# Gate and up products of the narrow expert slots with channels striped over four partition blocks and transposed in 32x32 blocks on VectorE; another order of the expert slots

## The chip, the cores and the metric

The kernel runs on one core of a Trainium2 chip. The metric is the device time of one execution in microseconds (us), lower is better. All matrices are in float32. PE is TensorE, DVE is VectorE, ACT is ScalarE, POOL is GpSimd, and SP is SyncE, whose queue issues the weight transfers.

## The reference

Two layers of a streaming encoder for 256 tokens with 1024 channels. Each layer mixes tokens (convolution and attention, then an output projection), then applies a feed-forward part. In the first layer that is a dense SwiGLU, in the second a mixture of eight experts of which each token uses two. The part that matters here is the second layer's:

```python
def moe_swiglu(h, w_router, b_router, w_gate, w_up, w_down):
    t = h.reshape(B * S, D)                       # 256 x 1024
    logits = t @ w_router + b_router
    top_val, top_idx = lax.top_k(logits, TOP_K)   # 2 of 8
    top_w = jax.nn.softmax(top_val, axis=-1)
    combine = sum(one_hot(top_idx, 8) * top_w)    # 256 x 8
    for e in range(8):
        # w_gate[e], w_up[e]: 1024 x 3584, w_down[e]: 3584 x 1024
        out += combine[:, e] * ((silu(t @ w_gate[e]) * (t @ w_up[e])) @ w_down[e])
```

## The kernel before, in words

The weights of the eight experts are 352 MB and pass through the chip once; each token goes only through its own two experts. The stage after the router is a list of **units** that Python writes out, and the order of that list is the order on every engine (`manual_schedule`).

**Slots.** Experts are put into eight slots by their number of tokens, at run time. Slot `e` has room for `32 * CAPS[e]` tokens, with `CAPS = (3, 4, 3, 3, 3, 2, 2, 2)`, so a slot has 2, 3 or 4 **groups** of 32 tokens. Slot 1 has 128 tokens and is called **wide**; the other seven are narrow. Each slot has seven units (`N_DN`), one for every 512 of the 3584 expert channels.

**Lanes.** `LANES` names two sequences of slots. The first three units of the first lane's first slot stand alone (`STAGGER`), then units of the first and second lane alternate, and the last three units of the second lane stand alone at the end. So a unit of one slot has a unit of another as its neighbour, and I write 3+2 for a pair of a three-group and a two-group unit.

**One unit** (the loop at the end of `moe`): `gu_mm` multiplies the tokens by 512 gate and 512 up channels, takes silu on ACT and multiplies on DVE; `dn_mm` multiplies the unit before it by its 512 rows of the down matrix; `h_T` transposes the unit's product, so that the next round's `dn_mm` can use it as the stationary operand. PE therefore runs: gate and up of unit n, down of unit n-1, transposes of unit n, gate and up of unit n+1.

**Narrow units** use PE in four strips of 32 columns (`streams`, line 1089): the 32 tokens of a group are the stationary operand, the weights are the moving one, and strip j takes a fourth of the channels and writes partitions 32j to 32j+31 of a PSUM bank. Strips run at the same time. In `gu_mm` one matmul has 128 gate and 128 up channels, 256 columns. The trace shows two records for a float32 matmul. Since a strip holds 128 neighbouring channels, the product must be transposed as a whole 128x128 square for each group: one PE transpose a group (line 1130) into a PSUM bank, and one ACT copy to SBUF (line 1137).

**The wide unit** splits its weights into two parts of fewer bits (line 140 on ACT and line 148 on DVE) and uses full 128x128 matmuls in three terms (lines 254 to 256).

**The weight stream.** A unit brings six tiles of 1 MiB (128x2048 float32): four of gate and up, two of down. `plan` lists them, SP issues them in that order (line 131), and each waits for its buffer to be freed. Near the wide slot tiles lie in the nine buffers of the pool `raw`. Elsewhere they also use the three buffers each of `hi` and `lo`, 15 in all. A narrow unit's tile is freed by the matmuls that read it, a wide one's by DVE's pass at line 148.

**Around the units.** Before a slot's first unit its tokens are gathered by matmuls (`dispatch`, lines 1025 to 1078); after its last one `gated` and `combine` scale the result and scatter it back (lines 1164 to 1200).

Of the kernel before, what the change touches and what calls it, by code (L numbers as in the profile page):

```python
# [13 lines left out]
AF = mybir.ActivationFunctionType  # L14
ALU = mybir.AluOpType
AX = mybir.AxisListType

P = 128
# [3 lines left out]
KT = 8  # L22
# [12 lines left out]
SPARE4 = (1, 6, 8)  # L35
EARLY = 7
CAPS = (3, 4, 3, 3, 3, 2, 2, 2)
LANES = (0, 2, 1, 3), (5, 4, 6, 7)
STAGGER = 3
NR = NE - 1  # L40
EPS = 1e-6
# [12 lines left out]
def kernel(ctx, tc, x, cvec, wada, bada, wga, wqkv, wout, wfgu, wfd, wfd2,  # L54
                      wmgu, wmd, cols, bias, wrt, brt, out):
    nc = tc.nc
# [10 lines left out]
    def bank(name):  # L67
        return pb.tile([P, 512], F32, tag="b", name=name)
# [6 lines left out]
    def sized(tag):  # L75
        def f(name, shape, dt=F32):
            return pools["wk"].tile(shape, dt, tag=tag, name=name, bufs=bufs[tag])
        return f

    a8, a4, a2 = sized("a8"), sized("a4"), sized("a2")  # L80
# [70 lines left out]
    plan = []  # L151
# [11 lines left out]
    first_gu = len(plan)  # L163
    runs = [[(e, c) for e in lane for c in range(N_DN)] for lane in LANES]
    units = runs[0][:STAGGER]
    for u in zip(runs[0][STAGGER:], runs[1]):
        units += u
    units += runs[1][-STAGGER:]
    after = {e: n for lane in LANES for e, n in zip(lane, lane[1:])}
    order = {0: 0}  # L170

    def of_slot(w, e, *parts):

        def f(c, h):
            v = w[0, c] if e == 0 else w[bass.ds(order[e], 1), c].rearrange("o p n -> (o p) n")
            return v[:, h * G:h * G + G]
        return lambda: [f(*p) for p in parts]

    def wide(e):
        return CAPS[e] == 4  # L180

    def down_chunk(e, c):
        return of_slot(wmd, e, (c, 0), (c, 1)), 4096 if wide(e) else 0

    for i, (e, c) in enumerate(units):
        parts = [[(2 * c + a, h) for h in range(2)] for a in range(2)]
        plan += [(of_slot(wmgu, e, *p), 4096 if wide(e) else 0) for p in (parts if wide(e) else zip(*parts))]
        if i:
            plan.append(down_chunk(*units[i - 1]))
    plan.append(down_chunk(*units[-1]))  # L190
# [36 lines left out]
    def blk(la=2, pre=True):  # L227

        i = used[0]
        used[0] += 1  # L230
        ahead(max(0, i + 1 + la - len(his)), max(0, i + 1 + la - len(los)), pre)
        return his[i], los[i]
# [674 lines left out]
    def moe(acc, g_bc, mm, A, B, AW, bw):  # L907
# [105 lines left out]
        def slot_pick(e):  # L1013
            src = places if e else posm
            return pick(lambda t: src[:, t, e:e + 1], 32 * CAPS[e])
# [68 lines left out]
        def streams(ps, g, x, w, first, last):  # L1084


            for t in range(g):
                for j in range(4):
                    nc.tensor.matmul(ps[t // 2][32 * j:32 * j + 32, t % 2], x(t), w(j),  # L1089
                                     start=first and t % 2 == 0, stop=last, skip_group_check=True)  # L1090

        def gu_mm(e, between):


            g, xg = CAPS[e], disp[e][0]
            ps = [bank(f"ps_gu{b}") for b in range((g + 1) // 2)]
            if wide(e):
                for b in range(2):
                    for s in range(2):
                        w = blk(min(2, 3 - 2 * b - s))  # L1100
                        for i in range(4):
                            k = 4 * s + i
                            mm3(ps[b], (xg[:, 0, k, :], xg[:, 1, k, :]), [v[:, 512 * i:512 * i + 512] for v in w],
                                k == 0, k == KT - 1)
                pv = [p_.rearrange("p (u t s) -> p t u s", t=2, u=2) for p_ in ps]
            else:
                pv = [p_.rearrange("p (t u s) -> p t u s", t=2, u=2) for p_ in ps]
                for h in range(2):
                    w = whole(3)
                    for i in range(4):  # L1110
                        k = 4 * h + i
                        wk_ = [w(a, i).rearrange("p (u j s) -> p u j s", u=2, j=2) for a in range(2)]
                        streams(pv, g, lambda t: xg[:, k, 32 * t:32 * t + 32], lambda j: wk_[j // 2][:, :, j % 2],
                                k == 0, k == KT - 1)
            between()
            sg = a2("sg", [P, g, P])
            hm = a2("mh", [P, g, P])
            for b, v in enumerate(pv):
                m = min(2, g - 2 * b)
                nc.scalar.activation(sg[:, 2 * b:2 * b + m, :], v[:, 0:m, 0, :], AF.Silu)  # L1120
            for b, v in enumerate(pv):
                m = min(2, g - 2 * b)
                nc.vector.tensor_tensor(hm[:, 2 * b:2 * b + m, :], v[:, 0:m, 1, :], sg[:, 2 * b:2 * b + m, :],  # L1123
                                        op=ALU.mult)
            return hm

        def h_T(hm, g, split=False):
            ps = bank("ps_hT").rearrange("p (a s) -> p a s", a=4)
            for t in range(g):
                nc.tensor.transpose(ps[:, t, :], hm[:, t, :], ident)  # L1130
            if split:
                hT = [a2(n, [P, g, P], F32R) for n in ("hThi", "hTlo")]
                nc.scalar.activation(hT[0], ps, AF.Copy)
                nc.vector.tensor_tensor(hT[1], ps, hT[0].bitcast(F32), op=ALU.subtract)
            else:
                hT = a2("hT", [P, g, P])
                nc.scalar.activation(hT, ps[:, 0:g, :], AF.Copy)  # L1137
            return hT
# [154 lines left out]
        with tc.manual_schedule():  # L1293
            limit[0] = len(halves)
            for r in range(NR):
                order[r + 1] = nc.values_load(idx_i[0:1, r:r + 1], engines=[mybir.EngineType.SP], min_val=1, max_val=NR,
                                              skip_runtime_bounds_check_because="a rank's expert")
            g2r = const.tile([P, 256], F32, tag="crep", name="g2r")
            pend, done = None, []
            for n, (e, c) in enumerate(units):  # L1300
                early = [(pe, gated(pe)) for pe in done]
                done = []
                if c == N_DN - 2 and e in after:
                    nxt = after[e]
                elif n == STAGGER - 1:
                    nxt = LANES[1][0]
                else:
                    nxt = None
                if nxt is not None:
                    pm = slot_pick(nxt)  # L1310

                def between():
                    if pend and wide(pend[0]):
                        ahead(2)

                hm = gu_mm(e, between)
                if n == 1:
                    g2_bc = bcast(vec(1, 5), "g2bc")
                    dgs = [a2("dg", [P, 4, P]) for i in range(2)]
                    for i, dg in enumerate(dgs):  # L1320
                        nc.vector.tensor_tensor(dg, ident[:, None, :].to_broadcast([P, 4, P]),
                                                vec(1, 5)[:, 4 * i:4 * i + 4, None].to_broadcast([P, 4, P]), op=ALU.mult)
                    ps = bank("ps_g2")
                    for j in range(4):
                        nc.tensor.matmul(ps[32 * j:32 * j + 32, 0:256], ones_1[:, 0:32],
                                         dgs[j // 2][:, 2 * (j % 2):2 * (j % 2) + 2, :].rearrange("p a s -> p (a s)"),
                                         start=True, stop=True)
                    nc.scalar.activation(g2r, ps[:, 0:256], AF.Copy)
                for pe, ys in early:
                    if pe == 0:  # L1330
                        macc = a8("macc", [P, NT, D])
                    combine(pe, ys)
                if pend is not None:
                    if pend[1] == 0:
                        accs[pend[0]] = [accbank(f"ps_d{b}") for b in range((CAPS[pend[0]] + 1) // 2)]
                    dn_mm(*pend)
                    if pend[1] == N_DN - 1:
                        done.append(pend[0])
                if n + 1 < len(units) and wide(units[n + 1][0]):
                    ahead(2)  # L1340
                pend = e, c, h_T(hm, CAPS[e], wide(e))
                if nxt is not None:
                    disp[nxt] = dispatch(nxt, pm)
            for pe in done:
                combine(pe, gated(pe))
            dn_mm(*pend)
            combine(pend[0], gated(pend[0]), store)
# [164 lines left out]
```

## Time and profile before

| | |
|---|---|
| median of three runs | 1421.37 us (1417.27 to 1430.04) |
| the profiled execution | 1421.24 us, its span 1419.2 us |
| PE, PE weight loads | busy 1349.9 us (95%), 973.1 us (69%) |
| DVE, ACT | busy 565.3 us (40%), 398.4 us (28%) |
| DMA | 473.64 MB, mean 334 GB/s |
| expert stage | from 519.2 us to the end of the span |

The span is the time from the first to the last instruction on the core. An engine's busy time is the sum over the span, so it mixes stages with different limits. Matmuls overlap, and the end of each is modelled, so a busy PE need not be at its peak; the start of one stream of matmuls to the start of the next is the better measure of its pace. A stretch in which the DMA engines are busy all the time and one in which PE is can follow one another within a stage, and only a view by stretches tells them apart.

### The profile page before, as it was taken

How to read it: one execution, taken by the hardware profiler on the slowest of the kernel's cores; microseconds unless marked ns; L12 is line 12 of the kernel's file. 1: busy time of each engine (PE TensorE's matmuls, PEld its weight loads, DVE VectorE, ACT ScalarE, POOL GpSimd, SP SyncE). 2: the span in 40 equal slices, each digit the busy share in tenths (PEclk: the TensorE clock that was granted, in tenths of full speed). 3: DMA queues.
4: the chain of work that ended last, by engine and by line, in shares of the span. 5: the costliest groups of instructions: out<-in, count | busy, mean ns of one | idle time of the engine just before them, and what ended most of it. 6: DMA issues, size and time to landing. Idle time of an engine off the chain costs nothing.

```text
span 1419.2 us, 38942 instructions
## 1 busy us (share of the span) xinstructions
PE 1349.9 (95%) x17604; PEld 973.1 (69%) x17604; DVE 565.3 (40%) x1025; ACT 398.4 (28%) x635; POOL 3.0 (0%) x17
## 2 busy tenths in 40 slices
PE   4998899999899999999999999999999999999886
PEld 4877699999697686657666656677667766665453
DVE  3597677777689651000100100354455430010011
ACT  3335444433456330101001001334333420100000
POOL 0000000000000000000000000000000000000000
PEclk9999999999999999999999999999999999999998
DMA  9963787878551579899999995989898999999995
GB/s 383 418 243 123 263 308 273 305 272 307 172 205 45 206 292 369 342 417 417 417 417 417 417 417 223 396 350 362 327 379 346 397 417 417 417 417 417 417 418 202
DMA packets 66379, 473.64 MB, mean 334 GB/s; under 512 B 7840, under 2 KB 7968, under 8 KB 9248
## 3 DMA queue, kind: packets, MB, share of 16 engines
q1 hardware_dynamic: 66208, 471.09, 83.3%
q8 instruction: 140, 2.29, 0.6%
q14 instruction: 31, 0.25, 0.0%
HBM read 470.01 MB, written 1.05 MB: 332 GB/s over the span
## 4 chain that ended last, share of the span: by engine, by line
PE 77%; DMA 13%; DVE 5%; ACT 3%; issue 1%; SPq 0%; DVEq 0%; ACTq 0%
PE ps_gu L1089 23%; PE ps_d L1089 13%; DMA raw<-in_wmgu 6%; DMA raw<-in_wmd 6%; PE ps_ga L256 4%; PE ps_ga L254 4%; PE ps_ga L255 4%; PE ps_g L1025 2%; PE ps_y L708 2%; PE ps_gu L256 2%; PE ps_gu L254 2%; PE ps_gu L255 2%; DVE cv L544 2%; PE ps_ada L308 1%; DVE lo L148 1%; PE ps_hT L1130 1%
## 5 line engine op out<-in xcount | busy, mean ns | idle before, releaser
L1089 PE MATMUL ps_gu<-raw,xn 128*32 128x256 f32 x8064 | 450.2, 380 | 4.1 <-DMA raw<-in_wmgu 3.9
L1089 PEld LDWEIGHTS ps_gu<-raw,xn 128*32 128x32 f32 x8064 | 269.1, 110 | 169.2 <-DMA raw<-in_wmgu 7.8
L148 DVE TENSOR_TENSOR lo<-raw,hi 128x2048 fp32r<-128x2048 f32 x99 | 225.5, 2289 | 84.7 <-ACT hi L140 82.0
L1123 DVE TENSOR_TENSOR mh<-ps_gu,sg 128x256 f32<-128x256 f32 (+1 forms) x91 | 32.7, 382 | 547.2 <-ACT sg L1120 547.2
L1089 PE MATMUL ps_d<-raw,hT 128*32 128x256 f32 x4032 | 232.3, 381 | 8.0 <-DMA raw<-in_wmd 7.5
L140 ACT ACTIVATE hi<-raw 128x2048 fp32r<-128x2048 f32 x99 | 188.3, 1912 | 107.2 <-PE ps_ga L256 43.0
L1089 PEld LDWEIGHTS ps_d<-raw,hT 128*32 128x32 f32 x4032 | 133.7, 110 | 96.6 <-DMA raw<-in_wmd 9.9
L1120 ACT ACTIVATE sg<-ps_gu 128x256 f32<-128x256 f32 (+1 forms) x91 | 32.0, 352 | 426.3 <-PE ps_gu L1089 380.7
L254 PE MATMUL ps_ga<-hThi,lo 128*128 128x256 f32 x480 | 137.5, 287 | 7.6 <-ACT hThi L446 7.6
L256 PE MATMUL ps_ga<-hTlo,hi 128*128 128x256 f32 x480 | 136.9, 285 | 0.8 <-DVE hTlo L451 0.8
L255 PE MATMUL ps_ga<-hThi,hi 128*128 128x256 f32 x480 | 136.3, 284 | 0.0
L254 PEld LDWEIGHTS ps_ga<-hThi,lo 128*128 128x128 f32 x480 | 92.9, 194 | 8.7 <-ACT hThi L446 8.4
L256 PEld LDWEIGHTS ps_ga<-hTlo,hi 128*128 128x128 f32 x480 | 92.4, 192 | 1.4 <-DVE hTlo L451 1.4
L255 PEld LDWEIGHTS ps_ga<-hThi,hi 128*128 128x128 f32 x480 | 92.4, 193 | 0.2
L544 DVE SCALAR_TENSOR_TENSOR cv<-zp,cols_sb,cv 128x256 f32<-128x256 f32 x206 | 85.4, 477 | 0.0
L1137 ACT ACTIVATE hT<-ps_hT 128x384 f32<-128x384 f32 (+1 forms) x49 | 21.8, 445 | 221.4 <-PE ps_hT L1130 221.4
L347 DVE SCALAR_TENSOR_TENSOR ada_acc<-raw,cs,ada_acc 128x512 f32<-128x512 f32 x63 | 47.2, 749 | 1.2
L256 PE MATMUL ps_gu<-lo,xg 128*128 128x512 f32 x112 | 44.3, 396 | 1.3 <-DVE lo L148 1.3
L254 PE MATMUL ps_gu<-hi,xg 128*128 128x512 f32 x112 | 44.8, 400 | 0.0
L255 PE MATMUL ps_gu<-hi,xg 128*128 128x512 f32 x112 | 44.3, 396 | 0.0
L308 PE MATMUL ps_ada<-raw,crep 128*32 128x128 f32 x960 | 34.4, 302 | 7.4 <-DMA raw<-in_wada 7.1
L308 PEld LDWEIGHTS ps_ada<-raw,crep 128*32 128x32 f32 x960 | 29.2, 121 | 11.2 <-issue 8.3
(263 smaller groups left out, 1310.1 us busy)
## 6 DMA issues: line engine op xcount, KB each, us to landing
raw<-in_wmgu SPq DMA_DIRECT2D x222, 1024.0 KB, 13.9
raw<-in_wmd SPq DMA_DIRECT2D x111, 1024.0 KB, 14.3
raw<-in_wada SPq DMA_DIRECT2D x48, 1024.0 KB, 6.2
raw<-in_wfgu SPq DMA_DIRECT2D x22, 1024.0 KB, 6.0
raw<-in_wqkv SPq DMA_DIRECT2D x12, 1024.0 KB, 6.6
raw<-in_wfd SPq DMA_DIRECT2D x11, 1024.0 KB, 6.5
raw<-in_wga SPq DMA_DIRECT2D x8, 1024.0 KB, 10.6
raw<-in_wout SPq DMA_DIRECT2D x8, 1024.0 KB, 7.7
```

The source lines that it names most:

```text
L140: nc.scalar.activation(hi[:, i * w:(i + 1) * w], r, AF.Copy)
L148: nc.vector.tensor_tensor(lo[:, w], r, hi[:, w].bitcast(F32), op=ALU.subtract)
L254: nc.tensor.matmul(o_, a[1], b[0], start=first, stop=False)
L255: nc.tensor.matmul(o_, a[0], b[0], start=False, stop=False)
L256: nc.tensor.matmul(o_, a[0], b[1], start=False, stop=last)
L308: nc.tensor.matmul(ps[32 * g:32 * g + 32, 0:P], crep[:, j, :], w(j)[:, g * P:(g + 1) * P], start=j == 0, stop=j == KT - 1)
L347: nc.vector.scalar_tensor_tensor(accs[ch], ws[ch](j), cs[:, j:j + 1], accs[ch], op0=ALU.mult, op1=ALU.add)
L544: nc.vector.scalar_tensor_tensor(cv[:, a, :], zp[:, a, i:i + S], cw[:, a, i:i + 1], cv[:, a, :], op0=ALU.mult, op1=ALU.add)
L708: nc.tensor.matmul(acc[t][hf], yf[:, k, t * P:(t + 1) * P], w(k // 2, 2 * (k % 2) + hf), start=k == 0, stop=False)
L1089: nc.tensor.matmul(ps[t // 2][32 * j:32 * j + 32, t % 2], x(t), w(j), start=first and t % 2 == 0, stop=last, skip_group_check=True)
L1120: nc.scalar.activation(sg[:, 2 * b:2 * b + m, :], v[:, 0:m, 0, :], AF.Silu)
L1123: nc.vector.tensor_tensor(hm[:, 2 * b:2 * b + m, :], v[:, 0:m, 1, :], sg[:, 2 * b:2 * b + m, :], op=ALU.mult)
```

## The change

Two things change. First, `LANES` is reordered: the wide slot is now second in its lane, and its neighbours are slots 5 and 6, with two groups each, where they were 4 and 6. Second, in narrow units a strip of PE takes, instead of 128 neighbouring channels, every fourth block of 32 channels. The product then lies so that transposing each 32x32 block in its place gives the layout that `dn_mm` wants. DVE does that in one instruction (`nc.vector.transpose`); the PE transposes and the ACT copy of narrow units go. A weight tile holds half of the 1024 rows for 256 gate and 256 up channels, so gate and up of a unit are done in two halves of the channels (`m`), each matmul now with 4 blocks of 32 columns, 128 columns, and there are twice as many. The two tiles of one load are now the two halves of the rows for the same channels (`parts`), where they were the same rows for two sets of channels (`zip(*parts)`). The wide unit is as before. Lines of the new kernel are up to 18 higher.

```diff
-LANES = (0, 2, 1, 3), (5, 4, 6, 7)
+LANES = (0, 1, 2, 3), (5, 6, 4, 7)
...
-        plan += [(of_slot(wmgu, e, *p), 4096 if wide(e) else 0) for p in (parts if wide(e) else zip(*parts))]
+        plan += [(of_slot(wmgu, e, *p), 4096 if wide(e) else 0) for p in parts]
...
             else:
-                pv = [p_.rearrange("p (t u s) -> p t u s", t=2, u=2) for p_ in ps]
-                for h in range(2):
+                pv = [p_.rearrange("p (t m a s) -> p t m a s", t=2, m=2, a=4) for p_ in ps]
+                for m in range(2):
                     w = whole(3)
-                    for i in range(4):
-                        k = 4 * h + i
-                        wk_ = [w(a, i).rearrange("p (u j s) -> p u j s", u=2, j=2) for a in range(2)]
-                        streams(pv, g, lambda t: xg[:, k, 32 * t:32 * t + 32], lambda j: wk_[j // 2][:, :, j % 2],
-                                k == 0, k == KT - 1)
+                    for k in range(KT):
+                        wk_ = w(k // 4, k % 4).rearrange("p (a j s) -> p j a s", a=4, j=4)
+                        streams([v[:, :, m] for v in pv], g, lambda t: xg[:, k, 32 * t:32 * t + 32],
+                                lambda j: wk_[:, j], m == 0 and k == 0, k == KT - 1)
+                between()
+                sg = a2("sg", [P, g, P])
+                hm = a2("mh", [P, g, P])
...
+                for b, v in enumerate(pv):
+                    n = min(2, g - 2 * b)
+                    nc.scalar.activation(sv[0][:, 2 * b:2 * b + n], v[:, 0:n, :, 0:64], AF.Silu)
+                for b, v in enumerate(pv):
+                    n = min(2, g - 2 * b)
+                    nc.vector.tensor_tensor(hv[0][:, 2 * b:2 * b + n], v[:, 0:n, :, 64:128],
+                                            sv[0][:, 2 * b:2 * b + n], op=ALU.mult)
+                hT = a2("hT", [P, g, P])
+                nc.vector.transpose(hT.rearrange("p t s -> p (t s)"), hm.rearrange("p t s -> p (t s)"))
+                return hT
...
-        def h_T(hm, g, split=False):
+        def h_T(hm, g, split=False, narrow=False):
+            if narrow:
+                return hm
...
-                pend = e, c, h_T(hm, CAPS[e], wide(e))
+                pend = e, c, h_T(hm, CAPS[e], wide(e), not wide(e))
```

How the instructions stand. On PE, around the second unit of slot 5 (two groups, its gate and up in one bank), before. `ps_gu` is gate and up, `ps_d` down, `x64` counts equal rows in a sequence:

```order
L1089 MATMUL ps_gu_5924<-raw,xn 32x256 x4
L1089 MATMUL ps_d_6035<-raw,hT 32x256 x32
L1130 MATMUL ps_hT<-ident,mh 128x128 x3
L1089 MATMUL ps_gu_6078<-raw,xn 32x256 x64
L1089 MATMUL ps_d_5319<-raw,hT 32x256 x8
```

The same place in the changed kernel:

```order
L1089 MATMUL ps_gu_6353<-raw,xn 32x128 x4
L1089 MATMUL ps_d_6562<-raw,hT 32x256 x32
L1089 MATMUL ps_gu_6599<-raw,xn 32x128 x128
L1089 MATMUL ps_d_5509<-raw,hT 32x256 x8
L1089 MATMUL ps_d_5510<-raw,hT 32x256 x4
```

A two-group unit has 128 gate and up matmuls of 128 columns where it had 64 of 256, the transposes between down and the next gate and up are gone, and the down matmuls are as they were. On PE behind the second wide unit, before (`hi`, `lo` and `xg` belong to the wide slot, `hT x4` are its transposes, which stay):

```order
L1089 MATMUL ps_d_8386<-raw,hT 32x256 x8
L1089 MATMUL ps_d_8387<-raw,hT 32x256 x4
L1130 MATMUL ps_hT<-ident,mh 128x128 x4
L1089 MATMUL ps_gu_9850<-raw,xn 32x256 x8
L1089 MATMUL ps_gu_9851<-raw,xn 32x256 x4
```

And in the changed kernel, behind its second wide unit:

```order
L256 MATMUL ps_gu_8099<-lo,xg 128x512
L1089 MATMUL ps_d_6562<-raw,hT 32x256 x32
L1148 MATMUL ps_hT<-ident,mh 128x128 x4
L1089 MATMUL ps_gu_8224<-raw,xn 32x128 x128
L254 MATMUL ps_d_8064<-hi,hTlo 128x512
```

The neighbour had three groups in two banks (`x8` and `x4` in turn) and now has two in one bank. On DVE, the first two units of the stage, before:

```order
L1123 TENSOR_TENSOR mh<-ps_gu_5084,sg 128x256
L1123 TENSOR_TENSOR mh<-ps_gu_5085,sg 128x128
L1123 TENSOR_TENSOR mh<-ps_gu_5194,sg 128x256
L1123 TENSOR_TENSOR mh<-ps_gu_5195,sg 128x128
L368 TENSOR_TENSOR dg<-ident,vcol 128x512 x2
```

And in the changed kernel:

```order
L1126 TENSOR_TENSOR mh<-ps_gu_5084,sg 128x256
L1126 TENSOR_TENSOR mh<-ps_gu_5085,sg 128x128
L1129 STREAM_TRANSPOSE hT<-mh 128x384
L1126 TENSOR_TENSOR mh<-ps_gu_5286,sg 128x256
L1126 TENSOR_TENSOR mh<-ps_gu_5287,sg 128x128
L1129 STREAM_TRANSPOSE hT<-mh 128x384
L368 TENSOR_TENSOR dg<-ident,vcol 128x512 x2
```

The transpose follows the two products of its unit directly, so everything that DVE does later stands behind it.

## Rows read from the trace of the kernel before

**Rows 1.** The page: head, and what the DMA moved in 40 slices.

```profile
span 1419.2 us, 38942 instructions
...
GB/s 383 418 243 123 263 308 273 305 272 307 172 205 45 206 292 369 342 417 417 417 417 417 417 417 223 396 350 362 327 379 346 397 417 417 417 417 417 417 418 202
```

**Rows 2.** Stretches: length, busy PE, PEld, DVE, ACT, POOL; PE clock, DMA share, GB/s.

```profile
519.20:603.00 83.80, 81.90 (x1443) 57.20 (x1446) 11.47 (x47) 11.30 (x27) 0.00 (x0) 1.00 0.91 365
603.00:852.00 249.00, 249.00 (x4538) 156.78 (x4534) 21.86 (x59) 25.28 (x65) 0.00 (x0) 1.00 1.01 417
852.00:1135.00 283.00, 280.19 (x3377) 196.61 (x3373) 119.51 (x110) 105.50 (x119) 0.00 (x0) 0.99 0.87 347
1135.00:1281.00 146.00, 146.00 (x2503) 90.27 (x2496) 21.14 (x39) 18.13 (x38) 0.00 (x0) 1.00 1.01 417
1281.00:1403.30 122.30, 110.21 (x1833) 61.85 (x1833) 8.54 (x18) 8.25 (x20) 0.00 (x0) 0.99 0.97 400
1403.30:1419.20 15.90, 5.89 (x94) 3.62 (x92) 4.05 (x7) 0.63 (x1) 0.00 (x0) 0.73 0.20 71
```

**Rows 3.** SP's issues in time: start, us, line, tile, count.

```profile
1180.30 7.85 SPq L131 DMA_DIRECT2D raw<-in_wmgu  x4
...
1364.53 7.82 SPq L131 DMA_DIRECT2D raw<-in_wmgu  x4
```

**Rows 4.** PE in time, three-group units after one another: start, us.

```profile
809.11 10.57 PE L1089 MATMUL ps_gu<-raw,xn 128*32 128x256 f32 x192
819.50 5.36 PE L1089 MATMUL ps_d<-raw,hT 128*32 128x256 f32 x96
824.79 0.55 PE L1130 MATMUL ps_hT<-ident,mh 128*128 128x128 f32 x3
825.27 10.57 PE L1089 MATMUL ps_gu<-raw,xn 128*32 128x256 f32 x192
```

**Rows 5.** PE in time, a pair 3+2 and the gathering behind it.

```profile
1177.73 0.40 PE L1089 MATMUL ps_d<-raw,hT 128*32 128x256 f32 x4
...
1178.43 10.57 PE L1089 MATMUL ps_gu<-raw,xn 128*32 128x256 f32 x192
...
1205.36 3.68 PE L1025 MATMUL ps_g<-pm,x_sb 128*128 128x64 f32 x32
...
1210.12 1.25 PE L1089 MATMUL ps_gu<-raw,xn 128*32 128x256 f32 x18
```

**Rows 6.** PE in time, the transposes one pair wide+2 apart.

```profile
1058.33 0.38 PE L1130 MATMUL ps_hT<-ident,mh 128*128 128x128 f32 x2
...
1086.76 0.38 PE L1130 MATMUL ps_hT<-ident,mh 128*128 128x128 f32 x2
```

**Rows 7.** The page, groups: count, busy us, mean ns, idle before.

```profile
L1089 PE MATMUL ps_gu<-raw,xn 128*32 128x256 f32 x8064 | 450.2, 380 | 4.1 <-DMA raw<-in_wmgu 3.9
...
L1089 PE MATMUL ps_d<-raw,hT 128*32 128x256 f32 x4032 | 232.3, 381 | 8.0 <-DMA raw<-in_wmd 7.5
...
L308 PE MATMUL ps_ada<-raw,crep 128*32 128x128 f32 x960 | 34.4, 302 | 7.4 <-DMA raw<-in_wada 7.1
```

**Rows 8.** Line 308: shortest, median and longest of one, ns.

```profile
L308 PE MATMUL ps_ada<-raw,crep x960: 272/273/423, 6.4 to 511.5; 128*32 128x128 f32 x192
```

**Rows 9.** PE in time, one adaLN product.

```profile
504.68 1.96 PE L308 MATMUL ps_ada<-raw,crep 128*32 128x128 f32 x64
```

**Rows 10.** Groups by form from 515 us on, two of DVE.

```profile
L1171 DVE TENSOR_TENSOR ylo<-yg,yhi 128x768 fp32r<-128x768 f32 x4 | 3.8, 958 | 3.6 <-ACT yhi L1170 3.6
...
L1048 DVE COPY xn<-xf 128x384 f32<-128x384 f32 x8 | 2.9, 360 | 23.1 <-ACT xf L1029 23.1
```

**Rows 11.** The page, DMA queue of instruction loads.

```profile
q8 instruction: 140, 2.29, 0.6%
```

**Rows 12.** PE in time, a scatter between two units.

```profile
697.77 0.50 PE L1195 MATMUL ps_sc<-yhi,pmT 32*128 32x256 f32 x4
...
700.47 3.66 PE L1089 MATMUL ps_d<-raw,hT 128*32 128x256 f32 x64
```

More of the change, by code (lines that the diff above doesn't have):

```diff
@@ L1106, in gu_mm @@
             else:
-                pv = [p_.rearrange("p (t u s) -> p t u s", t=2, u=2) for p_ in ps]
-                for h in range(2):
+                pv = [p_.rearrange("p (t m a s) -> p t m a s", t=2, m=2, a=4) for p_ in ps]
+                for m in range(2):
                     w = whole(3)
-                    for i in range(4):
-                        k = 4 * h + i
-                        wk_ = [w(a, i).rearrange("p (u j s) -> p u j s", u=2, j=2) for a in range(2)]
-                        streams(pv, g, lambda t: xg[:, k, 32 * t:32 * t + 32], lambda j: wk_[j // 2][:, :, j % 2],
-                                k == 0, k == KT - 1)
+                    for k in range(KT):
[5 more added lines that the diff above has]
+                hm = a2("mh", [P, g, P])
+                pv, sv, hv = ([v.rearrange("p (t m s) -> p t m s", t=n, m=2) for v in vs]
+                              for vs, n in ((ps, 2), ([sg.rearrange("p t s -> p (t s)")], g),
+                                            ([hm.rearrange("p t s -> p (t s)")], g)))
+                for b, v in enumerate(pv):
[8 more added lines that the diff above has]
+                return hT
             between()
```

## The prediction

> **What bounds the kernel now.** I read the slices first, then the stretches of the expert stage, then single units, and last the transfers. The slices [rows 1] show that from slice 17 to 23 and from slice 32 on the DMA moves 417 to 418 GB/s, and that between them it falls to 223 to 397. So the expert stage, from 519.2 us to the last weight at 1403.3, has two owners in turn: the weight stream and PE. [rows 2] gives this as a table. At 603 to 852 and 1135 to 1281 the DMA share is 1.01 and PE is never idle either; at 852 to 1135 the DMA moves 347 GB/s and PE is busy for 280.19 of 283 us; from 1281 PE loses 12.1 us of 122.3 to waits for weights.
>
> Who owns which stretch follows from pairs of units, since the two lanes alternate. A pair brings 12 tiles of 1 MiB. In the saturated stretch 72 of them were issued between the row at 1180.30 and the row at 1364.53 [rows 3]: 184.2/72 = 2.56 us each, 30.7 us a pair (410 GB/s; the 417 of [rows 2] also counts instruction loads and bytes of transfers that have not landed). PE without waits needs 16.16 us for a three-group unit (809.11 to 825.27 [rows 4]), so 32.3 for two of them; 26.93 for a three-group and a two-group unit (1178.43 to 1205.36 [rows 5]), so 10.77 for a two-group unit; 28.43 for a wide and a two-group unit (1058.33 to 1086.76 [rows 6]), so 17.66 for a wide one, and 33.8 for a wide and a three-group one. Against 30.7 us of DMA, pairs 3+3 and wide+3 belong to PE, pairs 3+2 and wide+2 to the DMA. In the old order four 3+3 and three wide+3 pairs follow one another; there the DMA fills its buffers (15 tiles, 9 near the wide slot) and stops. Afterwards only DMA-owned pairs are left, and the lost transfer time cannot be won back.
>
> **The ledger of the DMA.** Bytes from 519.2 to 1403.3 by [rows 2]: 30.6 + 103.8 + 98.2 + 60.9 + 48.9 = 342.4 MB. At 410 GB/s that is 835 us; the stretch took 884.1. The 49 us are 9.2 in the first 83.8 us, 43.5 in 852 to 1135, 3.0 at the end, less 6.8 in the two stretches at 417.
>
> **The change part by part.**
>
> *Order of the slots.* The wide unit now stands only beside two-group slots (5, then 6), and the 3+3 pairs, now seven (slots 2 and 3 beside 4), come later, with DMA-owned pairs before and after. PE needs 28.4 us for wide+2 and 26.9 for 3+2, under 30.7, so from the wide slot on the DMA should not find its buffers full. The 3+3 pairs exceed the DMA by 1.6 us each, 11 us over seven, plus two gatherings of some 5 us (4.76 for a two-group slot, 1205.36 to 1210.12 [rows 5]); 15 tiles are 38 us of stock, so they refill the stock and stop nothing. One stop I keep: entering the wide slot the stock falls from 15 tiles to 9, 15 us of transfers. Four 3+2 pairs stand before it, each 4 us quicker on PE than on the DMA, 16 us, less the wide slot's gathering of about 5: if the stock was full before them, 15 - 11 = 4 us remain. Bounds are 0 (stock already under 9 tiles) and 15 (stock full); I take 7, the middle. Of the 43.5 us 36.5 come back.
>
> *Gate and up matmuls of 128 columns.* Records of gate and up in the narrow slots go from 8064 to 16128, columns stay. Records come in fours (four column strips at once). Now one four of 256 columns takes (10.57 - 0.38 - 0.02)/47 = 216 ns (192 records in 48 fours; 0.38 is the last record [rows 7], 0.02 the spread of the four starts, from the four records in 0.40 at 1177.73 [rows 5]). The nearest row with 32 stationary and 128 moving columns is the adaLN product: 64 records, (1.96 - 0.27 - 0.02)/15 = 111 ns a four [rows 8, 9], a stretch of 1.7 us. Two fours are 222 against 216: +5.6 ns times 48 = 0.27 us a three-group unit, 0.18 a two-group one, 28 x 0.27 + 21 x 0.18 = +11 us of PE. The other end, from the busy sums [rows 7]: 34.4 us/960 = 35.8 ns a record against 450.2/8064 = 55.8, two for one +28%, or +122 us on the 436 us of gate and up (28 x 10.39, from 809.11 to 819.50 [rows 4], and 21 x 6.93, two thirds of it). That sum counts the drain after each short burst, which long streams do not have, so I take the first. The moving operand now comes in four pieces of 32 columns; today gate and up read two pieces of 128 and down one of 256, at 55.8 and 57.6 ns a record [rows 7], so one break costs nothing; three are not shown. The Trainium skill, "TensorE: Matmul & The Clock Gate", section "Back-to-back issue gap", gives some 81 ns per matmul at 128 columns and 131 at 512 in a stream of weight load and matmul pairs; as an estimate by that page two halves would cost 1.24 to 2 times the whole, and the kernel would end between some 1475 and 1800 us. The row of the adaLN product does not agree.
>
> *Transposes.* Off PE: the step between two streams is 0.2 us (end of gate/up to down in [rows 4]) and 0.79 with three transposes in it (last start 824.48 to 825.27); with two 0.68. Saved 0.59 x 28 + 0.48 x 21 = 27 us of PE, net of the 11 above 15 to 16. Off ACT: 49 copies, beside PE. On DVE: 49 transposes of 128x384 or 128x256. No row shows one; a plain copy of 128x384 takes 360 ns, a two-input pass of 128x768 958 [rows 10]; I take 0.45, nearest the copy of the same size, 22 us in all. DVE is busy 119.5 of 283 us in its fullest stretch [rows 2]. The transposed tile is read after the next unit's gate and up, 7 to 10 us later, so even 2 us is hidden; if that cover is gone (DVE late with the wide slot's low halves, which queue behind the transpose), PE waits some 2 us, most likely at a unit after a gathering, where the five small buffers have gone round and the transpose's is still read by a down product. The SP queue gets no new transfer; its order of two tiles in a gate/up load changes, which lets the first tile go a quarter of a unit after the start instead of half.
>
> *Instruction loads.* 16128 records of gate and up more, counting matmul and weight load, are 41% of the 38942 instructions [rows 1]; their queue took 0.6% of 16 engines' span [rows 11], 136 us of one engine, so 57 us more. Spread over all 16 engines that is 3.5 us of the stream, over eight 7; I take 5.
>
> **The sum.** PE alone: 28 x 16.16 + 21 x 10.77 + 7 x 17.66 = 802, seven gatherings (35), seven scatters of about 2.5 (2.7 at 697.77 to 700.47 [rows 12]) and a broadcast (4): 859 us, after the change 844, ending at 1363. The stream: 884.1 - 36.5 + 5 = 852.6, last weight at 1371.8. The stream is last by 8 us, PE waits for it at the end, and the tail of 15.9 us [rows 2] (a down product, the scatter, the store) stays. Span 1419.2 - 36.5 + 5 = 1387.7; the profiled execution took 1421.24, 2.0 more than its span, so **1390 us**, 31 under it. It stands 0.1 us from the median of the three runs, 1421.37, so the forecast is 2.2% under the median. Nothing before the expert stage changes.
>
> **The rivals.**
>
> *Half-width matmuls cost more than half.* For it: the 28% of the busy sums, three breaks in each moving row, twice as many instructions per us to be fetched than now. Against it: 111 ns a four. Place: gate and up of the 49 narrow units. Up to 8 us it is hidden under the stream; PE alone reaches today's 1403.3 at 40 us more, 9% of 436; from there on it is slower than before. At 28% PE alone is 844 + 111 = 955, ending at 1474, with 16 of tail and 2 outside the span 1492. The rule of the Trainium skill told above would lead here too. Chance 0.12, from 1405 to 1500.
>
> *The DMA still stops in the middle.* The wide slot has only nine tiles of stock, its tiles are freed by DVE's low-half pass (the stage's longest instruction there), and PE was for some us on the lower of its clocks there, 1.2 of 2.4 GHz (0.99 on average over 283 us [rows 2]), after a scatter. If such stops cost 10 to 20 us more, the end is 1400 to 1410. Against it: wide+2 leaves PE 2.3 us a pair of room. Chance 0.12.
>
> *No gain.* If the extra 57 us of instruction loading fall on one or two DMA engines, every tile waits for them: 28 to 57 us, and the time is 1413 to 1442. Against it: today's 136 us on one engine would leave no stretch at a share of 1.01. Chance 0.06.
>
> *The forecast*, 0.70: own range 1380 (no stop at the wide slot, 410 too low) to 1401.
>
> **How the numbers follow.** One per cent is 14 us, about what a measurement of this kernel can tell: under 1407 is faster. The forecast gives 0.69 of it and the second rival 0.09: 0.78. Within 1%: 0.01 of the forecast, 0.04 of the first rival, 0.03 of the second, 0.03 of the third: 0.11. Slower: 0.08 of the first, 0.03 of the third: 0.11. The range 1379 to 1410 holds the forecast, the second rival and the start of the first, about 0.8.
>
> **What would show it.** Right: no slice under 400 GB/s from the wide slot to the end but one at its entry; DMA share near 1 throughout; PE's waits for weights in the last 50 us; a four of 128 columns at 109 to 112 ns in a long stream; the transpose under 1 us. Wrong: PE never idle and the DMA again under 380 GB/s in the middle (the matmuls dearer); weight loads without a gap and matmul starts above 120 ns a four; tiles landing 2.7 us apart at a DMA share of 1 (instruction loads); waits of PE on DVE in the wide slot.

## The result and the profile after

The changed kernel is slower: 1575.6 us median of four runs (1565.49 to 1578.02) against 1420.53 (1417.27 to 1430.04) for the kernel before on the same chip, a ratio of 1.1072 [1.1009, 1.1134]. The forecast was 1390, the range 1379 to 1410. The profiled execution took 1575.11 us, 1.7 more than its span.

First the page of the changed kernel: head, GB/s of the slices, the queue of instruction loads (packets, MB, share of 16 engines), and the groups of the narrow units (busy us, mean ns of one, then the idle time ahead of them and what ended it). They answer to [rows 1, 7, 11].

```profile
span 1573.4 us, 54757 instructions
...
GB/s 387 416 139 218 256 313 287 292 297 185 161 110 171 309 242 316 362 341 256 362 393 416 376 371 394 416 344 354 302 315 301 317 275 292 302 322 378 338 376 63
...
q8 instruction: 202, 3.31, 0.8%
...
L1089 PE MATMUL ps_gu<-raw,xn 128*32 128x128 f32 x16128 | 493.4, 280 | 117.2 <-issue 117.2
L1089 PEld LDWEIGHTS ps_gu<-raw,xn 128*32 128x32 f32 x16128 | 466.7, 113 | 140.5 <-issue 136.5
...
L1089 PE MATMUL ps_d<-raw,hT 128*32 128x256 f32 x4032 | 244.8, 390 | 13.1 <-issue 12.9
```

The busy sum of gate and up rose by 43 us only, from 450.2 to 493.4. The loss stands in the last column: gate and up were preceded by 4.1 us of idle time, ended by a weight tile, and are now preceded by 117.2, ended by "issue". That word means that the engine waited for nothing the profile shows: no semaphore, no tile. The columns of the stretches are those of [rows 2]:

```profile
526.00:607.00 81.00, 67.67 (x1804) 59.45 (x1808) 12.27 (x49) 8.18 (x21) 0.00 (x0) 0.92 0.74 271
607.00:852.00 245.00, 222.74 (x4566) 185.57 (x4560) 77.92 (x86) 63.21 (x73) 0.00 (x0) 0.99 0.89 352
852.00:1135.00 283.00, 243.98 (x5374) 204.88 (x5368) 76.14 (x93) 52.98 (x69) 0.00 (x0) 0.98 0.94 371
1135.00:1281.00 146.00, 121.82 (x3426) 106.01 (x3418) 13.50 (x33) 7.93 (x23) 0.00 (x0) 0.96 0.79 294
1281.00:1557.50 276.50, 237.03 (x6475) 208.66 (x6479) 27.90 (x64) 12.64 (x36) 0.00 (x0) 0.95 0.82 311
1557.50:1573.40 15.90, 6.00 (x103) 4.61 (x93) 4.05 (x7) 0.63 (x1) 0.00 (x0) 0.73 0.20 71
```

Neither owner of the forecast is at its limit. Up to 1557.5 PE idles 9 to 17% of every stretch, where before it idled 10% in the last of them and under 3% in the others, and the DMA moves 271 to 371 GB/s where it moved 347 to 417. So something third stops PE, and the weight stream starves behind it, since PE frees the tiles.

PE in time shows what a stop looks like. Columns: start, us, instruction, count, and in brackets the idle time ahead of the row. The first rows are the very start of the expert stage, the later ones two three-group units of the saturated end.

```profile
526.62 2.17 PE L1089 MATMUL ps_gu<-raw,xn 128*32 128x128 f32 x70
530.41 3.70 PE L1089 MATMUL ps_gu<-raw,xn 128*32 128x128 f32 x128 [1.62 <-issue]
536.61 8.64 PE L1089 MATMUL ps_gu<-raw,xn 128*32 128x128 f32 x248 [2.50 <-issue]
...
1288.36 6.02 PE L1089 MATMUL ps_gu<-raw,xn 128*32 128x128 f32 x210
1296.63 3.70 PE L1089 MATMUL ps_gu<-raw,xn 128*32 128x128 f32 x128 [2.25 <-issue]
1302.84 1.39 PE L1089 MATMUL ps_gu<-raw,xn 128*32 128x128 f32 x42 [2.51 <-issue]
...
1309.15 6.93 PE L1089 MATMUL ps_gu<-raw,xn 128*32 128x128 f32 x243
1317.53 3.70 PE L1089 MATMUL ps_gu<-raw,xn 128*32 128x128 f32 x128 [1.45 <-issue]
1323.47 0.53 PE L1089 MATMUL ps_gu<-raw,xn 128*32 128x128 f32 x11 [2.24 <-issue]
```

Three times a row of exactly 128 matmuls stands between two stops. With their weight loads these are 256 instructions. Over the whole stage I counted, in the trace, 84 stops (more than 0.7 us from the start of one PE instruction to that of the next); 79 of them, 155.9 us in all, lie at the same place of the instruction stream, counted modulo 256. I call it the 256-place. The profile's own list of waits has most of this time ahead of the gate and up products (66 of the 79 stops stand there, ten ahead of down products, three ahead of scatters; that the first row also counts 79 is chance):

```profile
PEld ps_gu L1089 <- issue: 136.5, 79, 3.9
PE ps_gu L1089 <- issue: 117.2, 69, 3.6
```

The queue of instruction loads has the same step: 62 packets more (202 against 140) for 15815 instructions more (54757 against 38942), 255 each; 2.29 MB over 140 packets are 16.4 KB each. At every one of the 79 places such a load started 0.43 us before the stop on average, took 1.00 us, and PE went on 1.40 us (+-0.10) after its end. In the trace of before no stop lies at this place. **PE ran out of instructions.** A stream of 128 columns uses up 256 of them in 3.5 us (eight for every four of 109 ns), a stream of 256 columns in 6.9.

### The profile page after: what moved, and what is told of

Its sections match the earlier page's. It is cut to its first block, busy times and chain, and to the rows that moved or that the text cites. A ratio compares the mean times of both kernels' runs of the same rounds, so it can differ in the third digit from the quotient of the medians.

```text
span 1573.4 us, 54757 instructions
## 1 busy us (share of the span) xinstructions
PE 1381.5 (88%) x25542; PEld 1181.1 (75%) x25542; DVE 590.1 (38%) x1074; ACT 374.3 (24%) x586; POOL 3.1 (0%) x17
## 3 DMA queue, kind: packets, MB, share of 16 engines
HBM read 470.01 MB, written 1.05 MB: 299 GB/s over the span
## 4 chain that ended last, share of the span: by engine, by line
PE 82%; issue 10%; DVE 5%; ACT 3%; DMA 1%; SPq 0%; DVEq 0%; ACTq 0%
PE ps_gu L1089 30%; PE ps_d L1089 14%; PE ps_ga L256 3%; PE ps_ga L254 3%; PE ps_ga L255 3%; PE ps_g L1025 2%; PE ps_y L708 2%; PE ps_gu L256 2%; PE ps_gu L254 2%; PE ps_gu L255 2%; DVE cv L544 1%; PE ps_ada L308 1%; DVE lo L148 1%; PE ps_f L254 1%; PE ps_f L255 1%
## 5 line engine op out<-in xcount | busy, mean ns | idle before, releaser
L1089 PE MATMUL ps_gu<-raw,xn 128*32 128x128 f32 x16128 | 493.4, 280 | 117.2 <-issue 117.2
L1089 PEld LDWEIGHTS ps_gu<-raw,xn 128*32 128x32 f32 x16128 | 466.7, 113 | 140.5 <-issue 136.5
L1126 DVE TENSOR_TENSOR mh<-ps_gu,sg 128x256 f32<-128x256 f32 (+1 forms) x77 | 26.4, 372 | 652.8 <-ACT sg L1123 652.8
L1089 PE MATMUL ps_d<-raw,hT 128*32 128x256 f32 x4032 | 244.8, 390 | 13.1 <-issue 12.9
L1089 PEld LDWEIGHTS ps_d<-raw,hT 128*32 128x32 f32 x4032 | 158.3, 113 | 83.4 <-issue 27.7
L1123 ACT ACTIVATE sg<-ps_gu 128x256 f32<-128x256 f32 (+1 forms) x77 | 23.7, 344 | 711.4 <-PE ps_gu L1089 687.2
L254 PE MATMUL ps_f<-hi,hl 128*128 128x512 f32 x88 | 35.6, 404 | 0.0
```

The costliest lines, as they stand in the source:

```text
L254: nc.tensor.matmul(o_, a[1], b[0], start=first, stop=False)
L1126: nc.vector.tensor_tensor(hv[0][:, 2 * b:2 * b + n], v[:, 0:n, :, 64:128], sv[0][:, 2 * b:2 * b + n], op=ALU.mult)
```

## The experiments

Three readings of the result stood against each other first: the number of instructions, the moving operand in four pieces of 32 columns, and the new order. Medians are given with their count of runs, ratios against the kernel before on the same chip (1422.32, 1423.17 and 1421.52 us in the three sets).

### e1_split: the kernel before with two matmuls for each one of gate and up

```diff
-                        streams(pv, g, lambda t: ..., lambda j: wk_[j // 2][:, :, j % 2], k == 0, ...)
+                        for u in range(2):
+                            streams([v[:, :, u] for v in pv], g, lambda t: ...,
+                                    lambda j: wk_[j // 2][:, u, j % 2], u == 0 and k == 0, ...)
```

> The kernel before (old order, neighbouring channels, PE transposes), with one edit: each gate and up matmul of 256 columns is issued as two of 128, one over the gate columns and one over the up columns, each a single unbroken piece. The result is unchanged. Theory 1 (PE runs out of instructions: twice as many records a microsecond, loads of 256 cannot keep up): PE stands still with nothing to wait for at the end of every few loads of 256, some 120 us or more in all; 1540 to 1620 us. Theory 2 (moving rows in four pieces of 32 columns are slow): nothing is in such pieces here, so only the 11 us of shorter matmuls; 1420 to 1440 us. Theory 3 (the new order of slots costs the time) and theory 4 (VectorE's transpose makes PE wait): neither is here, 1420 to 1440 us.

Measured: 1628.73 us (4 runs, 1624.16 to 1636.95), 1.1445 [1.1388, 1.1501]: 9 us above the range of theory 1 and some 190 above those of the others. The page of this kernel:

```profile
q8 instruction: 203, 3.33, 0.8%
...
L1089 PE MATMUL ps_gu<-raw,xn 128*32 128x128 f32 x16128 | 489.4, 278 | 128.1 <-issue 127.8
```

Old order, old layout, unbroken columns, transposes on PE: only the matmuls are twice as many and half as wide, and the whole loss is there and more, with 85 stops (182.9 us) at the 256-place.

### e2_contig: the changed kernel with unbroken columns

```diff
-    ...rearrange("p (a j s) -> p j a s", a=4, j=4)
+    ...rearrange("p (j a s) -> p j a s", a=4, j=4)
```

> The changed kernel, with the moving operand of each gate and up matmul one unbroken piece of 128 columns instead of four pieces of 32; the number of matmuls stays. It takes the wrong channels, so the output is not the reference's. Theory 1: as the changed kernel, 1560 to 1590 us. Theory 2: 1385 to 1400 us. Theories 3 and 4: as the changed kernel, 1560 to 1590 us.

Measured: 1563.12 us (2 runs), 1.0979 [1.0928, 1.1031], 82 stops at the place, 155.8 us.

```profile
L1089 PE MATMUL ps_gu<-raw,xn 128*32 128x128 f32 x16128 | 494.2, 280 | 122.7 <-issue 122.6
```

The mean of 280 ns is that of the changed kernel to the nanosecond, and the time is 12 us (0.8%) shorter. The pieces cost no more than that.

### e3_order: only the new order

```diff
-LANES = (0, 2, 1, 3), (5, 4, 6, 7)
+LANES = (0, 1, 2, 3), (5, 6, 4, 7)
```

> The kernel before with the new order of the slots alone. Theory 1, and the ledger of the prediction for this part: the DMA no longer stops in the middle, but PE keeps its 859 us and so ends at about 1378 plus its waits; 1392 to 1405 us. Theory 3: the new order is what costs, 1500 us or more. Theories 2 and 4 say nothing against 1392 to 1405.

Measured: 1401.21 us (4 runs, 1397.79 to 1406.23), 0.9843 [0.98, 0.9885]. Its stretches:

```profile
603.00:852.00 249.00, 246.24 (x3051) 168.38 (x3050) 102.85 (x96) 88.87 (x98) 0.00 (x0) 0.99 0.97 394
852.00:1135.00 283.00, 283.00 (x4763) 182.33 (x4765) 45.79 (x77) 46.86 (x89) 0.00 (x0) 1.00 1.01 415
1135.00:1281.00 146.00, 146.00 (x2640) 94.15 (x2633) 14.15 (x36) 13.39 (x35) 0.00 (x0) 1.00 0.99 390
1281.00:1384.00 103.00, 102.52 (x1829) 60.88 (x1829) 8.54 (x18) 8.23 (x20) 0.00 (x0) 1.00 0.96 396
```

The middle stretch went from 347 [rows 2] to 415 GB/s: the order does what the ledger said. It gains 21 us and not 36, since PE, with its transposes still there, now idles for half a us in the three later stretches together and sets the end.

### e4_striped256: the whole change, with 256 columns in a matmul

The weights are laid out so that a tile has 1024 columns for each of two contraction rows in place of 512 for four. A strip then takes 8 blocks of 32 columns, and the instructions are as many as before.

```diff
-                pv = [p_.rearrange("p (t m a s) -> p t m a s", t=2, m=2, a=4) for p_ in ps]
+                pv = [p_.rearrange("p (t a s) -> p t a s", t=2, a=8) for p_ in ps]
...
-                    for k in range(KT):
-                        wk_ = w(k // 4, k % 4).rearrange("p (a j s) -> p j a s", a=4, j=4)
+                    for i in range(4):
+                        k = 4 * m + i
+                        wk_ = w(i // 2, 2 * (i % 2), 1024).rearrange("p (a j s) -> p j a s", a=8, j=4)
```

> The whole change, but with the weights laid out so that 1024 columns of one row of the contraction lie in one tile: a strip's gate and up matmul has again 256 columns, now in eight pieces of 32, and their number is that of the kernel before. Order of slots, VectorE transposes and output as in the changed kernel. Theory 1: no stops for instructions, the forecast of the prediction holds without the 11 us and the 5 us: 1378 to 1395 us. Theory 2: eight pieces are worse than four, over 1575 us. Theories 3 and 4: 1550 to 1580 us.

Measured: 1386.55 us (4 runs, 1383.76 to 1390.02), 0.9742 [0.9705, 0.978]: faster than both kernels. Its page:

```profile
GB/s 382 404 284 75 263 296 280 305 303 297 191 244 42 172 187 396 362 403 417 376 366 418 403 416 409 415 417 417 417 417 417 417 417 417 407 404 416 416 417 184
...
q8 instruction: 139, 2.28, 0.7%
...
L1089 PE MATMUL ps_gu<-raw,xn 128*32 128x256 f32 x8064 | 448.6, 379 | 1.6 <-DMA raw<-in_wmgu 0.9
```

and its longest stretch, columns as in [rows 2]:

```profile
700.00:1371.00 671.00, 662.05 (x10619) 431.46 (x10612) 170.78 (x234) 122.06 (x170) 0.00 (x0) 1.00 0.99 407
```

Order, striping and transposes on VectorE, all that the change is but the doubled instructions, give what was forecast. Of the idle time at "issue" ahead of gate and up, 0.5 us is left.

### e7_striped256_old: e4 in the old order

The edit is that of e4, and `LANES` as before.

> The kernel with striped channels, VectorE transposes and matmuls of 256 columns, in the old order of the slots, so that the order's share can be told from the transposes'. By theory 1 and the ledger PE alone loses 27 us of transposes, of which the stretch that PE owns gives back some; 1398 to 1408 us. If order and transposes were worth the same alone and together: 1422 - (1401 - 1387) = 1408 us.

Measured: 1408.62 us (4 runs), 0.99 [0.9884, 0.9917]. Striping and transposes alone are worth 14 us; the order adds 22 to them and 21 without them, so in kernels whose instructions come in time the two add up.

### e9_stripes_old: the whole change in the old order

```diff
-LANES = (0, 1, 2, 3), (5, 6, 4, 7)
+LANES = (0, 2, 1, 3), (5, 4, 6, 7)
```

> The whole change but in the old order of the slots. It tells what the order and the transposes are each worth once PE is stopped by its own instructions. Theory (PE's instruction loads come late, each stop some 1.8 us, and the weight stream is no longer the bound): going from the split kernel in the old order with transposes on PE (1628.7 us) to this one takes the transposes off PE, 27 us by the prediction's step, so 1600 to 1605; the rest to the changed kernel (1575.6) is then the order, as large as without the stops (21 to 22 us). About 80 to 92 stops at the same place. Rival (the order only helps a kernel that the stream bounds, which this one is not): 1575 to 1585, and the transposes were worth 45 us or more. A third reading, that the new order is what makes the stops: under 1500.

Measured: 1577.46 us (2 runs, 1573.37 to 1581.55), 1.1085 [1.1005, 1.1164], 77 stops at the place, 153.3 us. My theory fell here and the rival stands: with PE stopped by its instructions the order is worth nothing (1575.6 with it). Striping and taking the transposes off PE was worth 51 us here (from 1628.73): the prediction's 27 of PE time and 30 fewer of stops (182.9 to 153.3) would account for 57. Why the stops are fewer was not tested.

### e8_cols64: the kernel before with four matmuls of 64 columns for each one

```diff
+                        for u in range(2):
+                            for q in range(0, 128, 64):
+                                streams([v[:, :, u, q:q + 64] for v in pv], g, lambda t: ...,
+                                        lambda j: wk_[j // 2][:, u, j % 2, q:q + 64], u + q + k == 0, ...)
```

> The kernel before, with each gate and up matmul of 256 columns issued as four of 64: 32256 records instead of 8064, result unchanged. Theory 1: PE's time is the number of instructions by the pace of their loading. The stage has then some 75000 PE instructions, 293 loads of 256; the split into two showed one load in 6 to 7 us when PE was starved, so some 519 + 293 x 6.3 = 2350 us, between 2100 and 2600. By the column count alone, without starving: 1420 to 1470 us.

Measured: 2117.56 us (one run), at the lower edge of theory 1's range, 181 stops at the place, 521.6 us, 329 instruction loads. The stops are not all of the 694 us: PE's granted clock was 0.50 for 454 us of the stage, against 72 in the changed kernel. PE in time:

```profile
800.25 1.92 PE L1089 MATMUL ps_gu<-raw,xn 128*32 128x64 f32 x121
802.43 1.99 PE L1089 MATMUL ps_gu<-raw,xn 128*32 128x64 f32 x128 [0.26 <-issue]
808.64 6.31 PE L1089 MATMUL ps_gu<-raw,xn 128*32 128x64 f32 x256 [4.22 <-issue]
815.85 1.99 PE L1089 MATMUL ps_gu<-raw,xn 128*32 128x64 f32 x128 [0.90 <-issue]
822.07 3.64 PE L1089 MATMUL ps_gu<-raw,xn 128*32 128x64 f32 x128 [4.22 <-issue]
```

Behind the first row every piece is 128 matmuls or 256. PE runs through 256 instructions in 2 us and then stands for up to 4.22.

### Why the loads come late: e5_halfload, e10_quarterload, e6_small

A load takes 1.0 us and PE goes on 1.4 us later, which fits into 3.5 if the load starts early enough. In the changed kernel, though, the load ahead of a stop started 6.2 us after the one before it (median of 78). When a load starts can be counted in the traces: most stretches of PE from one 256-place to the next have one load (129 of 136 in the narrow units of the changed kernel), and it starts some time after PE has passed the first of the two places; where PE stops at the second, it stands until 1.4 us after that load's end. So no more than one block of 256 is in hand. In the narrow units of the kernel before the load starts 2.0 us after the place (median of 71), in those of the changed kernel 2.9 us. That makes 2.0 + 1.0 + 1.4 = 4.4 us where a block lasts 6.9, and 5.3 us where it lasts 3.5.

Either the weight stream delays the start of the loads, or the delay is fixed. e5_halfload and e10_quarterload load only the first half, or quarter, of the columns of each narrow tile (from the ninth pair of tiles of the stage on), and the matmuls read it two or four times; number, shape and order of the matmuls stay.

```diff
-                nc.sync.dma_start(r, src[:, o_:o_ + w])
+                if part:
+                    nc.sync.dma_start(r[:, 0:w // 2], src[:, o_:o_ + w // 2])     # w // 4 in e10
+                else:
+                    nc.sync.dma_start(r, src[:, o_:o_ + w])
```

> The changed kernel, but of each weight tile of the narrow slots only the first half of its columns is loaded, and the matmuls read that half twice, so half of the narrow slots' products is left out; all matmuls, their order and their number stay. The weight stream is no bound any more. Theory 1a (instruction loads come late because they wait among the packets of the weight stream): PE's stops at every 256th instruction vanish or shrink below 20 us in all, and PE alone is left: 1360 to 1400 us. Theory 1b (instruction loading has a pace of its own, whatever else the DMA engines do): the stops stay, 1530 to 1590 us.

Measured: 1455.64 us (2 runs), 1.023 [1.0187, 1.0272], 42 stops at the place, 60.2 us. That is in neither range: the stops shrink to four tenths and do not vanish.

```profile
L1093 PE MATMUL ps_gu<-raw,xn 128*32 128x128 f32 x16128 | 471.6, 274 | 48.8 <-issue 48.4
```

> The changed kernel, but of every narrow weight tile only the first quarter of the columns is loaded, and the matmuls read it four times; their number, shape and order stay. Half of the columns gave 1455.6 us with 42 stops of 60 us in all. If what makes an instruction load late is the weight stream beside it, a quarter of the stream leaves fewer still: under 15 stops, gate and up without 20 us of waits, and PE alone sets the end: 844 us from 519.2 by the prediction's sum, or 1363 and the tail of 16 and 2 outside the span, 1375 to 1400. If a part of the lateness is fixed (the load with its 1.0 us and the 1.4 us behind it, against 3.5 us that 256 instructions last), the stops stay at 35 to 50 and the time at 1440 to 1460.

Measured: 1412.59 us (4 runs, 1407.17 to 1413.41), 0.9924 [0.9882, 0.9965], 16 stops at the place, 24.3 us.

```profile
L1093 PE MATMUL ps_gu<-raw,xn 128*32 128x128 f32 x16128 | 463.0, 273 | 22.5 <-issue 22.1
```

With all, half and a quarter of the narrow tiles' bytes the stops are 156, 60 and 24 us, for the same 202 loads. The median interval of all loads in the stage falls from 6.0 to 4.7 and 4.3 us, the tenth that follows fastest comes 3.7, 3.5 and 3.5 us apart (3.5 is also what PE uses up). Counted from the 256-place the start falls from 2.9 to 1.7 and 1.1 us. So it is the weight stream that delays them. The changed kernel's own trace says the same: where weights moved at under 250 GB/s in the 3 us about the place, the load started 1.05 us after it (median of 25), at 400 and more 3.5 us (50). My floor of 15 stops and 1400 us was a little too low: at a quarter of the bytes 1.1 + 1.0 + 1.4 = 3.5 us just meet what a block lasts, so the later ones of the loads still stop PE. The stream's rate is not all of it: in the kernel before, at 400 GB/s and more, the loads started 2.0 us after the place and not 3.5. What makes this difference was not tested.

e6_small tests one way in which it might: the length of the transfers that wait in the queue. Each weight tile (of the wide slot too, from the seventeenth of the stage on) goes as four transfers of 256 KB.

```diff
-                nc.sync.dma_start(r, src[:, o_:o_ + w])
+                for q_ in range(0, w, 512):
+                    nc.sync.dma_start(r[:, q_:q_ + 512], src[:, o_ + q_:o_ + q_ + 512])
```

> The changed kernel with each weight tile brought by four transfers of 256 KB instead of one of 1 MB; bytes, buffers and matmuls stay. At most eight transfers are outstanding in the kernel before, so a quarter of the bytes stand in the queues. Theory 1a: a shorter queue lets an instruction load through sooner, the stops of PE halve at least: 1400 to 1500 us. Theory 1b: the stops stay, 1550 to 1600 us; more if the smaller transfers are slower by themselves.

Measured: 1557.77 us (2 runs), 1.0947 [1.0925, 1.0969], 90 stops at the place, 157.3 us, theory 1b's range. The size of a transfer isn't it, and theory 1b's reason, a pace that the stream leaves alone, fell with the two runs above. By which path the stream holds up the loads (the DMA engines, the memory, the order in which requests are served) stays open.

## Why the prediction was wrong

**The step that failed is "Instruction loads".** It counted the instructions rightly (41% more, and 57 us more of one DMA engine; 0.8% of 16 engines' 1573.4 us are 201, 65 more than the 136 of before) and priced them as bytes in the stream, 5 us; at PE, which now uses up a load in 3.5 us and not 6.9, it put them at nothing, without a reason. What they cost is their lateness at PE: 156 us of stops, and more by the clock. PE's granted clock stood at 0.50, the lower of its two levels, in 20 stretches between 526 and 1557 us, 72 us in all by my count, each of them behind idle time of PE, 19 of them behind such a stop. One of them, with the columns of [rows 2]:

```profile
640.00:643.20 3.20, 3.20 (x68) 3.20 (x64) 0.00 (x0) 0.00 (x0) 0.00 (x0) 0.50 0.66 207
```

A four of 128 columns takes 213 ns there (median) against 109 elsewhere, so of these 72 us, less 4 that lie in stops, nearly half are lost, 33.

With both the prediction's own sum closes. PE alone was to end at 1363; the stage began 7 us later in this execution (526.6 against 519.2); 156 of stops and 33 of clock make 1559; the tail of 16 and 2 outside the span make 1577. Measured: 1575.1. For e10_quarterload the same sum (24 of stops, 3 of clock) gives 1409, measured 1412.8.

**What of the trace of before could have told it.** [rows 11] with [rows 1] give 16.4 KB and 278 instructions (of all engines) a load, and the trace has the time of each load. In the expert stage of before they follow one another at a median of 7.3 us, since its matmuls need one each 6.9: this is the pace at which they were used, and it does not tell how fast they could come. Where they start tells more. The times of the loads against PE's instructions show one load for every 256 instructions of PE, started 2.0 us after PE passes one and the same place (half of them between 1.9 and 2.2) and landed 1.0 later. The 1.4 us until PE can use it show in no wait of before, but even without them 3.0 of the coming 3.5 us were gone, and nine loads in ten started 1.5 us after the place or later. The prediction bounded the pace of a matmul from both sides and not the pace at which matmuls are delivered.

The Trainium skill, "Trainium Architecture — The Big Picture", section "The software stack", says that an instruction has 64 bytes; this case's trace agrees, 1.02 MB more for 15815 more (64.5 bytes each).

**Order of the slots**: right. e3_order moves 415 GB/s where 347 were moved, and e4_striped256, which has every term of the sum but those of doubled instructions, ends at 1386.55; the prediction without its 5 us for instruction loads is 1385.

**Gate and up matmuls of 128 columns**: right. Between stops a four takes 109 ns (111 forecast), and e10_quarterload has 273 ns as the mean of one. The rule of the Trainium skill told in the prediction ("TensorE: Matmul & The Clock Gate", section "Back-to-back issue gap", 81 ns at 128 columns) is not what this trace shows for float32 matmuls in four column strips: four records start within 109 ns, 27 each.

**Transposes**: right, and slightly dearer than the 0.45 us taken. The line of VectorE (shortest, median and longest of one, ns):

```profile
L1129 DVE STREAM_TRANSPOSE hT<-mh x49: 445/578/580, 544.6 to 1555.3; 128x384 f32<-128x384 f32 x28, 128x256 f32<-128x256 f32 x21
```

The trace names nobody who waited for them.

**The rivals.** "Half-width matmuls cost more than half" had the side and, in half a sentence, the cause ("twice as many instructions per us to be fetched"). But it priced it at 28% of busy time, 1492 us, as if each matmul grew dearer. Each stayed as cheap; 156 and 33 us on 436 of gate and up are 43%, but the 156 stand in the idle column, and the 33 of the clock in the busy sum, which rose by 43. The stops of the DMA in the middle did come, but behind PE, not from the wide slot. The third rival, instruction loads on one or two DMA engines that hold up the tiles, had it the wrong way round: with fewer bytes of tiles the instruction loads come sooner (e5_halfload, e10_quarterload), so the tiles hold up the instruction loads.

## What to carry to other kernels

An engine has a supply of instructions, and a change that does the same work in twice as many has to be checked against it: divide the instructions by the packets of the instruction queue, see how long an engine takes for so many now and after the change, and compare with the time from the engine's entry into one block to the landing of the next, beside the same DMA traffic. The intervals between the loads say less, since an engine that is not short of instructions sets them itself. Idle time "<-issue" that recurs every 128 matmuls is the sign of it. If a layout halves the columns of a matmul, lay the weights out so that the columns stay (e4_striped256); and don't judge one part of a change, as the order here, in a kernel that another part has given a new bound.

## What the runs showed of the hardware

PE takes its instructions in blocks of 256 by DMA while the kernel runs, 16.4 KB a load. A load moves in 1.0 us and PE continues 1.4 us after it; its start follows PE's passing of the 256-place, so one block is all that covers it. The start came 2.0 us after the place in the kernel before, beside a full stream; in the changed kernel it came 2.9 us after it, 1.7 with half and 1.1 with a quarter of the narrow tiles' bytes (medians). A kernel of float32 matmuls in four strips uses a block up in 6.9 us at 256 columns, 3.5 at 128 and 2.0 at 64, and took 1422, 1629 and 2118 us with the same work, the same layout and the same order.
